# Six rows of the modulation leave the second half of the values and go to the output projection, whose last block gets a row beside each of six weight blocks

## The chip, the core and the metric

The kernel runs on one core of a Trainium2 chip. The metric is device time in microseconds (us) of one execution; lower is better. The engines are TensorE (PE; its weight loads are listed apart as PEld), VectorE (DVE), ScalarE (ACT), GpSimd (POOL) and SyncE (SP). Here SP issues nearly all loads, and POOL issues most stores. Every engine works through its own instructions in the order in which they were recorded, and waits on semaphores for the others; all DMAs of the core share 16 DMA engines.

## The reference

One layer of a diffusion backbone over 512 latent tokens with a prefix of 256 context tokens, width 2048. What matters here, cut down:

```python
mod_x = (silu(c) @ w_ada + b_ada)                       # 6 x 2048 numbers
sh1, s1, g1, sh2, s2, g2 = jnp.split(mod_x, 6, axis=-1)
h = rmsnorm(x, norm1_w) * (1 + s1) + sh1                # the same for the context
q, k, v (two kinds of heads) = projections of h         # v: "the values"
o = attention(q, k, v)                                  # 16 heads
x = x + g1 * (o @ w_o)                                  # "the output projection"
h2 = rmsnorm(x, norm2_w) * (1 + s2) + sh2
x = x + g2 * conv_ffn(h2)                               # w_up, convolution, SiLU, w_down
out = rmsnorm(x, final_w)
```

The modulation `mod_x` is a matrix times a vector: w_ada has 2048 x 12288 numbers, 100 MB, of which each is used once (a part also serves the context). All numbers are float32.

## The kernel before

**Matmuls.** Features lie on the 128 partitions, tokens along the free axis. A float32 product is made of three matmuls on rounded parts: ScalarE casts an operand to its high part (`wh`), VectorE subtracts that from the raw operand (`wr`) for the low part (`wl`), and TensorE adds high x high, high x low and low x high (lines 284 to 286, `mm3`). Weights come in blocks of 128 x 1024, 512 KB. Raw, high and low blocks have three buffers each, so that a load waits until the block three before it is cast and subtracted, and a cast until TensorE is done with the block three before.

**The modulation's rows.** The modulation isn't computed on TensorE but on VectorE, 128 features at a time. A "row" is one such piece: a load of 1024 KB of w_ada (128 x 2048, `ada`) and one instruction that multiplies it by silu(c), copied to all partitions (`cb`), and sums along it into one column of `modx`. There are 96 rows: 0 to 15 are sh1, 16 to 31 s1, 32 to 47 g1, 48 to 63 sh2, 64 to 79 s2, 80 to 95 g2. The rows of sh1 and s1 come first of all (those of s1 another way, through TensorE for both kinds of tokens). The rest is spread over later stages, always with two row buffers: a row's load waits until VectorE is done with the row two before it.

**Order of the stages, and where the rows are.**

1. Norms, first features, and the rows of sh1 and s1.
2. Features (keys, compressed queries): with each, 1 to 3 rows (`next_gemv`).
3. The values, in two halves of eight weight blocks (`values`). TensorE does 36 matmuls for a block; behind it come the cast and subtraction of a block for later, and then 0 to 2 rows on VectorE (`gate`), as a small table says. Each `gate` issues the load of one more row (`load_row`). The blocks that the second half loads last already belong to attention (`w_f`). At the end the results are split into two parts and written to DRAM, by POOL; the last four of these stores come out of the two row buffers, which are free by then.
4. Attention (`Flow`). A planner with a fixed table of due times orders the steps of all engines: loads of keys and values, projections of queries (`w_f` blocks, line 973 load, 985 cast, 986 subtraction), scores (line 1023), their maximum on VectorE (1026), the exponential on ScalarE (1028), the difference of the two maps (1177, 1178), rotary embedding (1124 to 1128), transposes and products with the values. At its end it also does the first quarter of the output projection.
5. The output projection `w_o`, in four groups of 512 features: group 0 within attention; groups 1 and 2 with one row for each of their 16 weight blocks (`next_gemv(wo, 1)`); and group 3, "the last block" of this document, eight weight blocks o0 to o7 written out by hand (`last_projection`) with no row before the change. For each of o0 to o5 TensorE does 24 matmuls, ScalarE casts the block after next (`cast(i + 2)`, line 1737), VectorE makes its low part (`low(i + 2)`, line 1745), which frees the raw buffer for another load (line 1558). o6 and o7 are done together, feature by feature, so that the next norm can begin.
6. The gated MLP: w_up, mostly by a recursion that saves multiplications, and w_down, to the end.

The stages 3, 4 and the last block onward are recorded by hand or by the planner: there the order on the engines is the order of the code. Groups 1 and 2 of the output projection stand outside, and the tile framework orders them.

**What reads the moved rows.** Rows 48 to 63 (sh2) are read in the second norm, after the last block; half of them also go into a small sum `db` (128 x 8), which was made on VectorE as soon as its inputs were there. g2 is read when w_down's first results come, g1 at the end of each group of the output projection.

Of the kernel before, what the change touches and what calls it, by code (L numbers as in the profile page):

```python
# [9 lines left out]
F32 = mybir.dt.float32  # L10
# [3 lines left out]
ALU = mybir.AluOpType  # L14
# [3 lines left out]
P = 128  # L18
D = 2048
# [201 lines left out]
def layer_kernel(ctx: ExitStack, tc: tile.TileContext, small, rope, c_row, cc_row, x_t, ctx_t, ada, ada_k,  # L221
                 w_g0, w_f, w_v, w_uqn, w_uqr, w_ukv, w_o, w_up0, w_up, w_dn, out_t):
    nc = tc.nc
    pe, ve, sc, gp = nc.tensor, nc.vector, nc.scalar, nc.gpsimd
# [8 lines left out]
    def nm(s):  # L233
        n[0] += 1
        return f"{s}{n[0]}"
# [64 lines left out]
    def col(name, j=0):  # L300
        o = OFF[name] + j
        return smt[:, o:o + 1]
# [8 lines left out]
    modx = cst.tile([P, 96], F32, name="modx")  # L311
# [52 lines left out]
    cb = st.tile([P, D], F32, name="cb")  # L364
# [6 lines left out]
    for j in (64, 96):  # L371
# [4 lines left out]
                            op1=ALU.mult)  # L376
# [3 lines left out]
    for i in range(2):  # L380
        o = OFF["lam"] + 128 * i
        ve.tensor_tensor_reduce(out=lt, in0=smt[:, o:o + 64], in1=smt[:, o + 64:o + 128], op0=ALU.mult,
                                op1=ALU.add, scale=1.0, scalar=0.0, accum_out=ls[:, i:i + 1])
# [64 lines left out]
    for p in range(8):  # L448
# [5 lines left out]
        def ctx_square(q=q, kts=kts, p=p):  # L454
            if p in ON_DVE:
                ve.tensor_tensor(hv(q(), kts, 1), cv(kts), cv(kts), op=ALU.mult)
            else:
# [3 lines left out]
             w=[q], hold=[cr[p // 2]])  # L461
# [34 lines left out]
    for k, (c0, c1) in enumerate(((0, T), (T, TT))):  # L496
# [13 lines left out]
            out=r, in0=nt[1]()[:, s], scalar=1.5, in1=r, op0=ALU.subtract, op1=ALU.mult), r=[nt[1]], w=[br])  # L510
# [222 lines left out]
    cb = kv.tile([P, D], F32, name="cb1")  # L733
# [2 lines left out]
    z = kv.tile([P, TT], F32, tag="lt", name=nm("z"), bufs=3)[:64]  # L736
    gp.memset(z, 0.0)
    gp.dma_start(zero_d, z)
    gv = iter([64 + i for i in range(16)] + [48 + i for i in range(16)] + [32 + i for i in range(16)])

    def next_gemv(pool, count):
        for _ in range(count):
# [159 lines left out]
    def values(half, vo):  # L902

        for kb in range(8):
            if half < 1 or kb < 7:
                raws.append(wload(next(wsrc)[0]))
            wh, wl = wready.pop(0)
            for j in range(2):
                kt = kb * 2 + j
                w = (wh[:, j * 512:(j + 1) * 512], wl[:, j * 512:(j + 1) * 512])  # L910
                order = (2, 3, 4, 5, 0, 1) if half and kt == KT - 1 else range(NKEY)
                for t in order:
                    src, o = (hx[kt], t * P) if t < 4 else (hc[kt], (t - 4) * P)
                    mm3(vo[t], (src[0][:, o:o + P], src[1][:, o:o + P]), w, kt == 0, kt == KT - 1)
            if not half and kb == 0:
                queries.pop(0)()
            wready.append(wsplit(raws.pop(0)))
            for _ in range(((2, 2, 2, 2, 2, 2, 2, 0), (2, 2, 2, 2, 2, 2, 1, 0))[half][kb]):
                gate()
            if queries and kb:  # L920
                queries.pop(0)()
        return order

    with tc.manual_schedule(engines={mybir.EngineType.PE, mybir.EngineType.Activation, mybir.EngineType.DVE,
# [4 lines left out]
        for half in range(2):  # L929
# [12 lines left out]
            for t in order:  # L942
                hl = []
                for _ in range(2):
                    if homes:
                        pool, g, bufs = homes.pop(0)
# [215 lines left out]
    for h in range(NH):  # L1162
        b, pace = BASE[h], SPANS[h] / 8
        ws = []
        for qt in range(NQT):
# [3 lines left out]
            for i in range(2):  # L1169
# [6 lines left out]
                out=second(), in0=rl()[:, 1:2], scalar1=neglam, scalar2=None, op0=ALU.mult), r=[rl], w=[second])  # L1176
            step("ACT", 0.85, t + 0.2, lambda p=ps[0], rl=rl: sc.mul(p(), p(), rl()[:, 0:1]), r=[rl], w=[ps[0]])
            step("DVE", 0.93, t + 1.2, lambda ps=ps, second=second: ve.scalar_tensor_tensor(
                out=ps[0](), in0=ps[1](), scalar=second(), in1=ps[0](), op0=ALU.mult, op1=ALU.add),
# [152 lines left out]
    for h in range(-1, NH):  # L1332
# [16 lines left out]
        p, i = h // 2, h % 2  # L1349
# [118 lines left out]
        ve.scalar_tensor_tensor(out=a2[:, dt:dt + 1], in0=modx[:, 64 + dt:65 + dt], scalar=1.0,  # L1468
                                in1=col("n2", dt), op0=ALU.add, op1=ALU.mult)
    db = sm.tile([P, 8], F32, name="db")  # L1470
    ve.tensor_tensor(db, modx[:, 56:64], modx[:, 48:56], op=ALU.add)

    HT = T // 2
    h0, h1 = slice(0, HT), slice(HT, T)
    halves = (h0, h1)
    x1, ss = [], wo.tile([P, T], F32, name="ss")
    gv = iter([80 + i for i in range(16)])

    def residual(dt):
        xr = wo.tile([P, T], F32, tag="xr", name=nm("xr"), bufs=4)  # L1480
        nc.sync.dma_start(xr, x_t[dt])
        x1.append(b2k())
        return xr
# [256 lines left out]
    def low(i):  # L1740
        if i < last and not kept_parts(i):
            hi, lo, raw, done = ready[i]
            n_ = 1024 // len(hi)
            for k, t in enumerate(lo):
                ve.tensor_tensor(t, raw[:, k * n_:k * n_ + n_], hi[k].bitcast(F32), op=ALU.subtract)  # L1745
            if done:
                done()
# [3 lines left out]
        return [tuple(h[j // k][:, j % k * P:j % k * P + P] for h in ready[i][:2]) for j in range(8)]  # L1751


    def last_projection(i):
        kb, w = jobs[i][1], [h[0] for h in ready[i][:2]]
        if kb < 6:
            for j in range(2):
                for d in range(4):
                    project(live["o"], d, kb * 2 + j, w, kb == 5 and j == 1 and d == 3)
            cast(i + 2)  # L1760
            low(i + 2)
            return
        outs, xr = live["o"], live["xr"]

# [341 lines left out]
    with tc.manual_schedule(engines={mybir.EngineType.PE, mybir.EngineType.Activation, mybir.EngineType.DVE,  # L2106
                                     mybir.EngineType.SP}):
        mem["ra"] = Ring(wp, "wr", 3, items_a)
        live["o"] = [b_tile() for _ in range(4)]
        live["xr"] = [residual(12 + d) for d in range(4)]  # L2110
        for i in range(2):
            cast(i)
            low(i)
        for i, job in enumerate(jobs):
            if job == ("n", 0):
                ps_b.release()
                ps_s.release()
                nb[0] = 3
                ps_b = tc.alloc_tile_pool(name="ps_m", bufs=3, space=PSUM, reuse_waits="tile")
                spare += [tp.tile([P, T], F32R, tag="tp", name=nm("tp")) for _ in range(8)]  # L2120
            {"o": last_projection, "n": first_tiles, "u": third_tile, "p": strassen, "d": strassen,
             "f": last_output}[job[0]](i)
# [86 lines left out]
```

## Time and profile before

| | |
|---|---|
| time, median of 3 runs | 2344.87 us (2342.84 to 2345.27) |
| the profiled execution's own time | 2342.02 us |
| its span (first to last instruction) | 2340.2 us |
| granted TensorE clock, mean | 0.993 of full |
| busy: PE, DVE, ACT, POOL | 2291.9, 1731.4, 1165.5, 268.0 us |
| DMA | 404.23 MB, mean 173 GB/s |
| values, second half | to about 423 us |
| output projection, last block | about 921 to 966 us |

How to read the rows that follow. The **page** lists each engine's busy time and share of the span. The list of **waits** has: who waited, for whom, us in total, times, the longest. A **timeline** row has: start, duration, engine, line, operation, tiles (written <- read), shape, count, and in brackets the engine's idle time before it and what ended that; SPq is SyncE issuing a DMA. A row of **windows** has: the stretch, its length, then for PE, PEld, DVE, ACT and POOL the busy time and (instructions), and at last the granted clock, the busy share of the DMA engines and GB/s. The **chain of waits** follows the work that ended last back from the end; its rows have start, duration and what the time went to, a DMA's from its issue to its landing. Rows of **groups** have a count, total busy time, mean ns of one, idle time before them. Rows of **DMA issues** end with KB of each and the median us from issue to landing.

### The profile page before, as it was taken

How to read it: one execution, taken by the hardware profiler on the slowest of the kernel's cores; microseconds unless marked ns; L12 is line 12 of the kernel's file. 1: busy time of each engine (PE TensorE's matmuls, PEld its weight loads, DVE VectorE, ACT ScalarE, POOL GpSimd, SP SyncE). 2: the span in 40 equal slices, each digit the busy share in tenths (PEclk: the TensorE clock that was granted, in tenths of full speed). 3: DMA queues.
4: the chain of work that ended last, by engine and by line, in shares of the span. 5: the costliest groups of instructions: out<-in, count | busy, mean ns of one | idle time of the engine just before them, and what ended most of it. 6: DMA issues, size and time to landing. Idle time of an engine off the chain costs nothing.

```text
span 2340.2 us, 32196 instructions
## 1 busy us (share of the span) xinstructions
PE 2291.9 (98%) x12378; PEld 1961.0 (84%) x12378; DVE 1731.4 (74%) x2206; ACT 1165.5 (50%) x1777; POOL 268.0 (11%) x308
## 2 busy tenths in 40 slices
PE   6999999899999999999999999999999999999998
PEld 4788888788888888898888888888888888888887
DVE  7988776698987776597685858585858585767667
ACT  6542211477767522455454545454545454545456
POOL 0000001100123222000101010101010101010110
PEclk8999999999999999999999999999999999999999
DMA  9978889745301197334647374646464555555573
GB/s 356 366 256 311 306 296 333 236 130 167 123 29 41 55 353 277 98 106 138 144 121 165 103 173 115 160 119 153 127 146 132 137 143 144 132 148 126 154 184 104
DMA packets 124731, 404.23 MB, mean 173 GB/s; under 512 B 14337, under 2 KB 18945, under 8 KB 114081
## 3 DMA queue, kind: packets, MB, share of 16 engines
q1 hardware_dynamic: 96658, 346.92, 44.4%
q0 software_dynamic: 26768, 54.21, 12.6%
q8 instruction: 97, 1.59, 0.3%
q10 hardware_dynamic: 1152, 1.05, 0.1%
q14 instruction: 56, 0.46, 0.1%
HBM read 332.45 MB, written 69.67 MB: 172 GB/s over the span
## 4 chain that ended last, share of the span: by engine, by line
PE 86%; DMA 5%; DVE 5%; issue 2%; ACT 1%; SPq 0%; POOL 0%; DVEq 0%; ACTq 0%; POOLq 0%
PE y L1921 13%; PE b L284 10%; PE b L285 10%; PE b L286 10%; PE y L1923 7%; PE z L1921 6%; PE s L1023 4%; PE z L1923 3%; PE x L1921 3%; DMA ada<-in_ada 2%; PE s L284 2%; PE s L286 2%; PE s L285 2%; PE x L1923 2%; PE f L284 2%
## 5 line engine op out<-in xcount | busy, mean ns | idle before, releaser
L1745 DVE TENSOR_TENSOR wl<-wr,wh 128x1024 fp32r<-128x1024 f32 x144 | 176.6, 1226 | 159.8 <-ACT wh L1737 159.1
L1942 POOL DMA_DIRECT2D x_d<-xs x160 | 139.8, 1001 | 1147.5 <-ACT xs L1941 1145.6
L1737 ACT CAST wh<-wr 128x1024 fp32r<-128x1024 f32 x144 | 150.9, 1048 | 217.0 <-PE b L285 117.9
L284 PE MATMUL b<-ah,wh 128*128 128x512 f32 (+1 forms) x664 | 256.8, 387 | 0.0
L285 PE MATMUL b<-al,wh 128*128 128x512 f32 (+1 forms) x664 | 256.7, 387 | 0.0
L286 PE MATMUL b<-ah,wl 128*128 128x512 f32 (+1 forms) x664 | 255.8, 385 | 0.0
L1745 DVE TENSOR_TENSOR wl<-rb,wh 128x1024 fp32r<-128x1024 f32 x123 | 150.1, 1220 | 121.0 <-ACT wh L1737 121.0
L1745 DVE TENSOR_TENSOR wl<-ws,wh 128x1024 fp32r<-128x1024 f32 x123 | 150.4, 1222 | 109.9 <-ACT wh L1737 109.9
L1737 ACT CAST wh<-rb 128x1024 fp32r<-128x1024 f32 x123 | 129.3, 1051 | 181.7 <-PE b L285 76.2
L1921 PE MATMUL y<-a2k,wh 128*128 128x512 f32 x656 | 164.0, 392 | 0.0
L1737 ACT CAST wh<-ws 128x1024 fp32r<-128x1024 f32 x123 | 128.5, 1044 | 68.5 <-PE b L285 48.5
L286 PEld LDWEIGHTS b<-ah,wl 128*128 128x128 f32 x664 | 124.8, 188 | 25.7
L284 PEld LDWEIGHTS b<-ah,wh 128*128 128x128 f32 x664 | 125.1, 188 | 22.9
L285 PEld LDWEIGHTS b<-al,wh 128*128 128x128 f32 x664 | 125.1, 188 | 21.9
L248 ACT CAST wh<-wr 128x1024 fp32r<-128x1024 f32 x51 | 53.5, 1052 | 169.4 <-DMA wr<-in_w_o 49.5
L1921 PEld LDWEIGHTS y<-a2k,wh 128*128 128x128 f32 x656 | 118.6, 189 | 21.6
L1026 DVE TENSOR_REDUCE m<-s 128x1 f32<-128x768 f32 x96 | 91.2, 952 | 25.5 <-PE s L1023 25.2
L1028 ACT ACTIVATE p<-s,m 128x768 f32<-128x768 f32 x96 | 86.8, 904 | 42.5 <-DVE m L1026 40.2
L352 DVE CUSTOM_DVE_ANT_0 ada<-ada,cb,smt 128x2048 f32<-128x2048 f32 x37 | 90.0, 2433 | 24.1 <-DMA ada<-in_ada 24.0
L1921 PE MATMUL y<-b2k,wh 128*128 128x512 f32 x410 | 106.8, 390 | 0.0
L1941 ACT ACTIVATE xs<-b,modx 128x512 f32<-128x512 f32 x160 | 101.2, 681 | 2.4 <-DMA x_d<-xs 2.1
L1923 PEld LDWEIGHTS y<-a2k,wl 128*128 128x128 f32 x656 | 89.5, 190 | 6.4
(528 smaller groups left out, 5943.8 us busy)
## 6 DMA issues: line engine op xcount, KB each, us to landing
ada<-in_ada SPq DMA_DIRECT2D x80, 1024.0 KB, 7.2
rb<-in_w_up SPq DMA_DIRECT2D x123, 512.0 KB, 4.4
wr<-in_w_dn SPq DMA_DIRECT2D x88, 512.0 KB, 3.8
x_d<-xs POOLq DMA_DIRECT2D x160, 256.0 KB, 6.0
wr<-in_w_up SPq DMA_DIRECT2D x53, 512.0 KB, 4.2
wr<-in_w_f SPq DMA_DIRECT2D x34, 512.0 KB, 6.8
adak<-in_ada_k SPq DMA_DIRECT2D x32, 512.0 KB, 7.7
wr<-in_w_o SPq DMA_DIRECT2D x32, 512.0 KB, 6.4
```

The source lines that it names most:

```text
L284: pe.matmul(out, st[0], mv[0], start=start, stop=False, **kw)
L285: pe.matmul(out, st[0], mv[1], start=False, stop=False, **kw)
L286: pe.matmul(out, st[1], mv[0], start=False, stop=stop, **kw)
L352: ve.tensor_tensor_reduce(out=junk, in0=w, in1=vec, op0=ALU.mult, op1=ALU.add, scale=1.0, scalar=col("b_ada", j), accum_out=dst[:, j:j + 1])
L1023: pe.matmul(s()[:, c0:c1], a, b[:, c0:c1], start=i == 0, stop=i == len(ms) - 1)
L1026: step("DVE", 0.87, t + cost + 0.2, lambda: ve.tensor_reduce(out=m(), in_=s()[:, :TT], axis=AX.X, op=ALU.max, negate=True), r=[s], w=[m])
L1737: sc.copy(t, raw[:, k * n_:k * n_ + n_])
L1745: ve.tensor_tensor(t, raw[:, k * n_:k * n_ + n_], hi[k].bitcast(F32), op=ALU.subtract)
L1921: pe.matmul(o, w[j][0], hs[j], start=start and j == 0, stop=False, skip_group_check=True)
L1923: pe.matmul(o[:, h0], w[j][1], hs[j][:, h0], start=False, stop=j == 7, skip_group_check=True)
L1941: sc.mul(x, po, modx[:, 80 + dt:81 + dt])
L1942: gp.dma_start(x1_d[dt], x, accum_op=ALU.add)
```

## The change

Three things move.

1. In the second half of the values the table of rows per block goes from 2, 2, 2, 2, 2, 2, 1, 0 to 2, 2, 2, 1, 0, 0, 0, 0. The list of rows for these stages loses rows 58 to 63.
2. The list for the output projection starts with these six rows, and then has g2's sixteen. The 16 blocks of groups 1 and 2 thus take rows 58 to 63 and 80 to 89, and six rows, 90 to 95, are left for the last block.
3. The last block gets two new helpers. `late_row` issues a load, `late_gate` does a row on VectorE and then issues another load. Two loads are issued ahead of o0, and one `late_gate` follows the subtraction in each of o0 to o5. The sum `db` is written down later, just ahead of the last block.

```diff
-    gv = iter([64 + i for i in range(16)] + [48 + i for i in range(16)] + [32 + i for i in range(16)])
+    gv = iter([64 + i for i in range(16)] + [48 + i for i in range(10)] + [32 + i for i in range(16)])
...
-            for _ in range(((2, 2, 2, 2, 2, 2, 2, 0), (2, 2, 2, 2, 2, 2, 1, 0))[half][kb]):
+            for _ in range(((2, 2, 2, 2, 2, 2, 2, 0), (2, 2, 2, 1, 0, 0, 0, 0))[half][kb]):
                 gate()
...
     db = sm.tile([P, 8], F32, name="db")
-    ve.tensor_tensor(db, modx[:, 56:64], modx[:, 48:56], op=ALU.add)
...
-    gv = iter([80 + i for i in range(16)])
+    gv = iter([58 + i for i in range(6)] + [80 + i for i in range(16)])
+    late_rows = []
...
+    def late_row():
+        j = next(gv, None)
+        if j is not None:
+            w = wo.tile([P, D], F32, tag="ada", name=nm("ada"), bufs=2)
+            nc.sync.dma_start(w, ada[j])
+            late_rows.append((j, w))
+
+    def late_gate():
+        j, w = late_rows.pop(0)
+        ve.tensor_tensor_reduce(out=w, in0=w, in1=cb, op0=ALU.mult, op1=ALU.add, scale=1.0,
+                                scalar=col("b_ada", j), accum_out=modx[:, j:j + 1])
+        late_row()
+
     def last_projection(i):
         kb, w = jobs[i][1], [h[0] for h in ready[i][:2]]
         if kb < 6:
...
             cast(i + 2)
             low(i + 2)
+            late_gate()
             return
...
         mem["ra"] = Ring(wp, "wr", 3, items_a)
         live["o"] = [b_tile() for _ in range(4)]
         live["xr"] = [residual(12 + d) for d in range(4)]
+        ve.tensor_tensor(db, modx[:, 56:64], modx[:, 48:56], op=ALU.add)
+        late_row()
+        late_row()
```

On TensorE, ScalarE and POOL the instructions stand in the same order as before. Three places differ.

SyncE at the end of the values, before: the last loads of rows (`ada`), of the values' and attention's first weight blocks, and then attention's first loads (`klz`, `qs`, `ks`).

```order
L893 DMA ada_3166<-in_ada 128x2048
L257 DMA wr_3168<-in_w_v 128x1024
L893 DMA ada_3211<-in_ada 128x2048
L893 DMA ada_3214<-in_ada 128x2048
L257 DMA wr_3216<-in_w_f 128x1024
L893 DMA ada_3259<-in_ada 128x2048
L257 DMA wr_3262<-in_w_f 128x1024
L1087 DMA klz_3394<-zero_d 64x768
L1097 DMA qs_3407<-q_d 128x512
```

The same place now:

```order
L257 DMA wr_3161<-in_w_v 128x1024
L257 DMA wr_3203<-in_w_f 128x1024
L257 DMA wr_3245<-in_w_f 128x1024
L1087 DMA klz_3376<-zero_d 64x768
L1097 DMA qs_3389<-q_d 128x512
```

The weight blocks follow each other directly, with no row's load, and so no wait for VectorE's rows, between them and ahead of attention's loads.

SyncE at the last block, before: the last of four loads of the residual (`xr`), then the weight blocks from o3 to the first of w_up.

```order
L1481 DMA xr_8441<-in_x_t 128x512
L1558 DMA wr_8448<-in_w_o 128x1024
L1558 DMA wr_8454<-in_w_o 128x1024
L1558 DMA wr_8484<-in_w_o 128x1024
L1558 DMA wr_8514<-in_w_o 128x1024
L1558 DMA wr_8544<-in_w_o 128x1024
L1558 DMA wr_8574<-in_w_up 128x1024
```

The same place now:

```order
L1481 DMA xr_8422<-in_x_t 128x512
L1758 DMA ada_8426<-in_ada 128x2048
L1758 DMA ada_8428<-in_ada 128x2048
L1558 DMA wr_8434<-in_w_o 128x1024
L1558 DMA wr_8440<-in_w_o 128x1024
L1558 DMA wr_8470<-in_w_o 128x1024
L1758 DMA ada_8473<-in_ada 128x2048
L1558 DMA wr_8503<-in_w_o 128x1024
L1758 DMA ada_8506<-in_ada 128x2048
L1558 DMA wr_8536<-in_w_o 128x1024
L1758 DMA ada_8539<-in_ada 128x2048
L1558 DMA wr_8569<-in_w_up 128x1024
```

Two rows stand ahead of o3, o4 and o5, and one each ahead of o6, o7 and the first two w_up blocks.

VectorE at the last block now, from the last eviction of group 2 (`b2k`) and the low parts of o2 to o5 (`wl`):

```order
L1487 SCALAR_TENSOR_TENSOR b2k_8395<-s_8104,modx,xr_8393 128x512
L1745 TENSOR_TENSOR wl_8467<-wr_8407,wh_8466 128x1024
L1763 ISA ada_8426,modx<-ada_8426,cb_7759,smt 128x2048
L1763 ISA modx 128x1
L1745 TENSOR_TENSOR wl_8500<-wr_8434,wh_8499 128x1024
L1763 ISA ada_8428,modx<-ada_8428,cb_7759,smt 128x2048
L1763 ISA modx 128x1
L1745 TENSOR_TENSOR wl_8533<-wr_8440,wh_8532 128x1024
```

Before, these subtractions followed each other with nothing between them; now a row (two instructions, the second stores the sum) stands behind each.

## The prediction

> **What bounds the kernel now.** The page first: TensorE is busy for 98% of the span, so only time in which TensorE waits, or runs at a lower clock, can be won. The list of TensorE's waits names one after the start-up phase that is longer than 2 us, and the table by windows puts it where the second half of the values hands over to attention:
>
> ```profile
> PE 2291.9 (98%) x12378; PEld 1961.0 (84%) x12378; DVE 1731.4 (74%) x2206; ACT 1165.5 (50%) x1777; POOL 268.0 (11%) x308
> PE s L1023 <- ACT p L1028: 6.0, 1, 6.0
> 400.00:410.00 10.00, 10.00 (x45) 8.27 (x45) 6.80 (x8) 1.06 (x1) 0.00 (x0) 1.00 0.90 325
> 430.00:440.00 10.00, 7.75 (x38) 6.34 (x36) 5.68 (x9) 3.61 (x7) 3.33 (x5) 1.00 1.03 397
> 443.00:444.00 1.00, 0.26 (x1) 0.26 (x2) 0.28 (x2) 0.69 (x2) 0.01 (x1) 0.50 1.01 399
> 448.00:449.00 1.00, 1.00 (x3) 0.74 (x3) 0.97 (x2) 1.00 (x3) 0.00 (x0) 0.50 0.07 16
> ```
>
> The last three columns are the granted clock, the DMA engines' share and GB/s. Up to 437 us TensorE is full while the DMA engines are full too; then it stands, and after the wait it runs at half clock. The timelines of TensorE and ScalarE and the chain of waits name the cause:
>
> ```profile
> 437.47 0.28 PE L1023 MATMUL s<-klz,qs 128*128 128x256 f32 x1
> 443.74 0.80 PE L1023 MATMUL s<-ks,qs 128*128 128x512 f32 x1 [6.00 <-ACT p L1028]
> 449.89 0.39 PE L1023 MATMUL s<-ks,qs 128*128 128x512 f32 x1
> 452.64 0.39 PE L1023 MATMUL s<-ks,qs 128*128 128x512 f32 x1
> ...
> 411.38 1.06 ACT L248 CAST wh<-wr 128x1024 fp32r<-128x1024 f32 x1 [8.21 <-DMA wr<-in_w_f]
> 435.52 0.93 ACT L1177 ACTIVATE p<-p,rl 128x768 f32<-128x768 f32 x1
> 441.75 1.04 ACT L985 CAST wh<-wr 128x1024 fp32r<-128x1024 f32 x1 [5.31 <-DMA wr<-in_w_f]
> 442.70 0.90 ACT L1028 ACTIVATE p<-s,m 128x768 f32<-128x768 f32 x1
> 444.59 0.90 ACT L1028 ACTIVATE p<-s,m 128x768 f32<-128x768 f32 x1 [0.90 <-DVE rt L1128]
> 447.60 0.90 ACT L1028 ACTIVATE p<-s,m 128x768 f32<-128x768 f32 x1
> ...
> 426.34 15.39 DMA wr<-in_w_f
> ```
>
> The exponential p (L1028) frees the scores' bank, but stands on ScalarE behind the cast of a w_f block, and that block takes 15.39 us to land. It is issued late and lands late because the queue was behind. SyncE's timeline:
>
> ```profile
> 400.89 2.75 SPq L893 DMA_DIRECT2D ada<-in_ada  x2
> 408.48 0.33 SPq L893 DMA_DIRECT2D ada<-in_ada  x1
> 409.40 0.52 SPq L1087 DMA_DIRECT2D klz<-zero_d  x1
> 426.34 2.76 SPq L973 DMA_DIRECT2D wr<-in_w_f  x2
> ```
>
> Attention's first load (409.40) stands behind the last gate row (408.48), which waits until VectorE has emptied a row buffer.
>
> **The change in the second half of the values: the wait.** It takes away six gate rows, 1024 KB and one VectorE instruction each:
>
> ```profile
> L898 DVE CUSTOM_DVE_ANT_0 ada<-ada,cb,smt 128x2048 f32<-128x2048 f32 x27 | 63.3, 2350 | 16.6 <-DMA ada<-in_ada 16.4
> ```
>
> VectorE's 6 x 2.35 = 14.1 us are worth nothing as such, since TensorE has 10.00 of 10 us in that stage. What counts is the queue: 6 x 1.049 = 6.3 MB, at the 325 GB/s of 400 to 410 us 19 us of transfers. With nothing waiting for rows, the two w_f blocks and attention's loads leave as soon as casts free their buffers, which TensorE paces; I estimate 10 to 15 us sooner. The block of 426.34 takes the buffer of the first w_f block, so its load can leave once that one is cast; that cast (411.38) waited 8.21 us for DMA, and when TensorE alone paces it, is due by 407 (the values end at 423; 36 matmuls to a block at 45 per 10 us are 8 us, and the cast may start two blocks before the end). The block is then there well before 436.45, when ScalarE (435.52 + 0.93) is free for its cast.
>
> Sum for this place. (a) From the cast's start to TensorE's restart it was 443.74 - 441.75 = 1.99 us; from 436.45 that gives 438.44, so 5.30 us are saved and 0.7 us of waiting stays. (b) Half clock: from 443.74 to 449.89 TensorE did one set of scores and 12 projection matmuls; one set and 9 matmuls at full clock are 452.64 - 449.89 = 2.75 us, with three more of 0.23 us 3.45. It took 6.15: 2.70 saved. (c) Given back: the neighbours rested during the wait and now are tight. VectorE:
>
> ```profile
> 439.27 0.69 DVE L1124 TENSOR_TENSOR rt<-f,ropet 128x512 f32<-128x512 f32 x1 [1.00 <-DMA v_d<-v]
> 441.25 0.95 DVE L1026 TENSOR_REDUCE m<-s 128x1 f32<-128x768 f32 x1
> ```
>
> L1124 writes where the values lay and waits for their store; without that 1.00 us the maximum (L1026) ends at 441.2, its exponential starts at 441.25 and TensorE's next scores at 442.3 (1.04 us from exponential to scores, 442.70 to 443.74). TensorE would be there at 438.44 + 3.45 = 441.9: 0.4 us of waiting. The next exponential follows 3.01 us later (444.59 to 447.60), scores 2.75 us later: 0.25 more; VectorE's chain to the one after, with a subtraction and three products ahead of its maximum, adds about 0.3 (an estimate). Together 0.95. Net 5.30 + 2.70 - 0.95 = 7.05 us. Bounds: 8.7 if nothing is left (6.00 + 2.70); 2.6 if only the last row's 1.05 MB at 397 GB/s comes off the block's landing and the half clock stays.
>
> **The clock.** A wait of 1.02 us elsewhere left the clock alone, 6.00 us did not:
>
> ```profile
> 967.85 0.70 PE L1809 MATMUL s<-sq,ones 128*128 128x256 f32 x2 [1.02 <-ACT sq L1773]
> 966.00:968.00 2.00, 0.98 (x8) 0.77 (x8) 1.89 (x5) 0.77 (x2) 0.36 (x1) 1.00 0.00 0
> ```
>
> The remaining 0.7 us is nearest the first, so (b) counts in full. [...]
>
> **The change in the output projection: the cover.** Rows 58 to 63 take the places of six gate-2 rows in the two middle blocks one for one (nothing there changes), so six rows come new into the last block, o0 to o7, one behind each of o0 to o5. Two are issued ahead of the loop, in front of o3's weights. What stands there now:
>
> ```profile
> 930.17 1.05 ACT L1737 CAST wh<-wr 128x1024 fp32r<-128x1024 f32 x1 [6.42 <-DMA wr<-in_w_o]
> 931.90 1.05 ACT L1737 CAST wh<-wr 128x1024 fp32r<-128x1024 f32 x1 [0.67 <-PE b L286]
> 937.14 1.05 ACT L1737 CAST wh<-wr 128x1024 fp32r<-128x1024 f32 x1 [4.20 <-PE b L285]
> 942.59 1.05 ACT L1737 CAST wh<-wr 128x1024 fp32r<-128x1024 f32 x1 [4.38 <-PE b L285]
> ...
> 931.25 1.23 DVE L1745 TENSOR_TENSOR wl<-wr,wh 128x1024 fp32r<-128x1024 f32 x1 [7.08 <-ACT wh L1737]
> ...
> 860.00:870.00 10.00, 10.00 (x46) 8.29 (x45) 6.18 (x6) 2.11 (x2) 0.00 (x0) 1.00 0.98 375
> 905.00:910.00 5.00, 5.00 (x24) 4.14 (x23) 4.36 (x4) 1.06 (x1) 0.00 (x0) 1.00 1.02 403
> 920.00:925.00 5.00, 5.00 (x24) 4.14 (x23) 3.12 (x3) 2.77 (x4) 4.97 (x5) 1.00 0.93 299
> ...
> ada<-in_ada SPq DMA_DIRECT2D x80, 1024.0 KB, 7.2
> ```
>
> A block is 5.45 us (937.14 to 942.59). o3's weights arrive at 930.17, their low part is ready at 932.48 and first read in o3's third matmul, about 937.8: 5.3 us of slack. Two rows are 2.1 MB, 5.2 us at 403 GB/s, and some of it fits into 920 to 925, where only 299 were moved. So o3 just arrives: 0 us, 1.2 us if the rows run at 325 GB/s. Behind it each block adds 2.35 us to VectorE's 1.23, 3.6 of 5.45 us. On VectorE the next block's subtraction stands behind each row, and two blocks later TensorE needs it; on SyncE o6, o7 and the first w_up blocks stand behind the loads of rows 3 to 6, needed at 942.59 and then 5.45 us apart. Two buffers bring two rows per 7.2 + 2.35 = 9.55 us, 4.8 per row, under 5.45. The row of 860 to 870 is this same load (one row, one block) with TensorE at 10.00. I take 0, nearest that row; bounds 0 and 13.8 (D).
>
> From 919 to 954 us the stage now moves 6.3 MB (four 256 KB loads and stores each, eight weight blocks); with the rows 12.6 MB in 35 us, 360 GB/s. [...] The sum db moves on VectorE and costs 0.17 us in cover of either stage.
>
> **Sum.** The profiled execution took 2342.02 us, 1.8 around its span; 2342.0 - 7.0 = 2335.0. It lies 2.85 under the median of the runs, so that the median becomes 2344.87 - 7.0 = 2337.9.
>
> **The rivals.**
> B, the backlog goes only in part: 2.6 us, 2342.3. For it: attention's own loads and the values' stores fill the engines too (397 GB/s from 430 to 440, when no row is left). Against: two of the six rows' loads were issued at 400.89 and one at 408.48, right ahead of them.
> C, a new wait takes the old one's place. The second exponential (444.59) writes into the freed row buffers, which still hold values on their way out; POOL stores them last:
>
> ```profile
> 430.77 0.75 POOL L955 DMA_DIRECT2D v_d<-ada  x1 [3.29 <-DMA v_d<-nr]
> 434.23 0.75 POOL L955 DMA_DIRECT2D v_d<-ada  x1 [0.33 <-issue]
> v_d<-ada POOLq DMA_DIRECT2D x4, 256.0 KB, 10.1
> ```
>
> 434.23 + 10.1 = 444.3, so this store, not L1128, ends that wait. Unchanged it would hold the scores to 445.6, 4.3 us before the old 449.89; 1.6 with half clock. Say 3: 2341.9. Against: the stores queue behind the same backlog, and are needed only by 441.2.
> D, slower: in the last block the two row buffers fall into step, so that rows 3 to 6 come one per 9.55 us and each holds VectorE's subtraction: 4 x (9.55 - 5.45) = 16.4, less the 5.3 of slack, plus 2.7 at half clock: 13.8 - 7.05 = 6.7 slower, 2351.6. It decides once a row takes over 2 x 5.45 - 2.35 = 8.55 us to land. Against: 7.2 is the median, and from 860 to 870 this load cost TensorE nothing.
> E, nothing: SyncE's order, and casts that TensorE paces, hold the w_f block, and it lands no sooner: 2344.9. Against: the cast that frees its buffer waited 8.21 us for DMA itself.
>
> **How the numbers follow.** Forecast 0.74, B 0.08, C 0.08, D 0.05, E 0.05. The forecast's own range is 5.5 to 8.7 us, 2336.2 to 2339.4, and with the runs' spread (2342.84 to 2345.27) 2335.0 to 2340.6. Stretched over B's and C's centres: 2335.0 to 2342.6. What can be told from no change is 0.2%, 4.7 us: faster 0.74 (the forecast, whose own range begins above it), same 0.21 (B, C, E), slower 0.05 (D).
>
> **What would show it.** Right: no L1023 wait over 1 us between 430 and 460, granted clock 1.00 there, DMA share well under 1 before 420, the second L985 cast waiting on no DMA; and TensorE at 10.00 per 10 us through the last block, with o3's cast some 4 us later. Wrong: a wait on v_d stores at the second exponential (C), a w_f cast still idle on DMA (B, E), or TensorE waiting for L1737 or L1745 (D).

## The result, and the profile after

| | before | after |
|---|---|---|
| median | 2342.84 us (7 runs, 2339.07 to 2348.64, measured beside the change) | 2333.48 us (7 runs, 2332.54 to 2337.57) |
| profiled execution | 2342.02 us, span 2340.2 | 2333.48 us, span 2331.6 |
| granted clock, mean | 0.993 | 0.995 |

The ratio is 0.996, with a 95% interval of 0.9948 to 0.9972: faster by 7 to 12 us. The prediction had 2337.9 (2335.0 to 2342.6): the direction is right, the size is not. One run of before, among those measured beside the experiments, took 4242.98 us at a granted clock of 0.807 and is left out everywhere.

The page of the profile after, a row of its list of TensorE's waits and its table by windows:

```profile
PE 2289.3 (98%) x12378; PEld 1958.4 (84%) x12378; DVE 1729.4 (74%) x2206; ACT 1164.8 (50%) x1777; POOL 267.4 (11%) x308
PE s L1023 <- ACT p L1028: 0.7, 1, 0.7
400.00:410.00 10.00, 10.00 (x46) 8.29 (x45) 1.22 (x1) 1.05 (x1) 0.00 (x0) 1.00 1.04 226
430.00:440.00 10.00, 9.13 (x44) 7.31 (x43) 7.29 (x13) 6.13 (x11) 0.94 (x2) 1.00 0.00 1
440.00:460.00 20.00, 19.81 (x99) 16.22 (x98) 18.97 (x28) 16.45 (x30) 1.13 (x4) 1.00 0.41 112
```

The wait of 6.0 us at the scores is 0.7 us, the clock stays at full, and from 430 to 440 us, where 397 GB/s were moved before, the DMA engines have nothing left to do. A new wait of 0.5 us stands in the last block (L1745, shown further below). From 400 to 410 us the DMA engines are as full as ever (1.04): what changed is what they carry. Timelines of after, SyncE, POOL, ScalarE and TensorE, and a row of its DMA issues:

```profile
392.27 0.52 SPq L1087 DMA_DIRECT2D klz<-zero_d  x1
408.62 6.57 SPq L973 DMA_DIRECT2D wr<-in_w_f  x2
424.77 2.98 POOL L955 DMA_DIRECT2D v_d<-ada  x4
433.67 1.04 ACT L985 CAST wh<-wr 128x1024 fp32r<-128x1024 f32 x1
434.70 0.90 ACT L1028 ACTIVATE p<-s,m 128x768 f32<-128x768 f32 x1
435.74 0.50 PE L1023 MATMUL s<-ks,qs 128*128 128x512 f32 x1 [0.68 <-ACT p L1028]
439.75 0.39 PE L1023 MATMUL s<-ks,qs 128*128 128x512 f32 x1
...
v_d<-ada POOLq DMA_DIRECT2D x4, 256.0 KB, 4.0
```

Attention's first load leaves at 392.27 (before: 409.40), the w_f block at 408.62 (426.34). Its cast at 433.67 waits for nothing. The values' last stores, which POOL had to issue from 430.77 to 434.23, leave together from 424.77 on and take 4.0 us instead of 10.1.

Where the 8.6 us between the spans are: I compare the start of the same matmul in both profiles. Late in the start-up, in code that the change doesn't touch, in before and in after; then, in after, the last matmul ahead of the scores that waited (437.47 in before):

```profile
155.43 2.08 PE L839 MATMUL s<-c4k,wl 128*128 128x256 f32 x16
...
152.75 2.08 PE L839 MATMUL s<-c4k,wl 128*128 128x256 f32 x16
434.78 0.28 PE L1023 MATMUL s<-klz,qs 128*128 128x256 f32 x1
```

At 155 us after leads by 2.68 us already (437.47 - 434.78 = 2.69 just ahead of the hand-over). At the scores that waited, its lead is 443.74 - 435.74 = 8.00; at the next it is 449.89 - 439.75 = 10.14, and 9.87 is left at 446 us of after. So the hand-over brought 7.18 us, and 2.69 came from the start-up. The rest of attention and the two middle groups take 0.20 us of it in small pieces: at 927 us of after the lead is 9.67. Then the last block takes some back. The matmul that read o3's low part, before, and the rows around it after (SyncE, the first row on VectorE, o3's cast and low part, TensorE, a window, and the row of the chain of waits):

```profile
937.63 0.39 PE L286 MATMUL b<-a2k,wl 128*128 128x512 f32 x1
...
913.20 1.01 SPq L1758 DMA_DIRECT2D ada<-in_ada  x2
914.32 1.68 SPq L1558 DMA_DIRECT2D wr<-in_w_o  x3
922.28 2.35 DVE L1763 CUSTOM_DVE_ANT_0 ada<-ada,cb,smt 128x2048 f32<-128x2048 f32 x1 [7.79 <-DMA ada<-in_ada]
926.32 1.05 ACT L1737 CAST wh<-wr 128x1024 fp32r<-128x1024 f32 x1 [12.25 <-DMA wr<-in_w_o]
927.41 1.23 DVE L1745 TENSOR_TENSOR wl<-wr,wh 128x1024 fp32r<-128x1024 f32 x1 [2.76 <-ACT wh L1737]
928.69 0.50 PE L286 MATMUL b<-a2k,wl 128*128 128x512 f32 x1 [0.53 <-DVE wl L1745]
915.00:920.00 5.00, 5.00 (x23) 4.14 (x23) 0.00 (x0) 0.00 (x0) 2.46 (x3) 1.00 0.87 285
914.32 11.93 DMA wr<-in_w_o
```

The two rows issued at 913.20 take until 922 and beyond, at 285 GB/s, and o3's weights behind them 11.93 us. The low part comes 0.53 us late by the row, and the lead falls to 937.63 - 928.69 = 8.94 at once and to 8.81 with the next matmuls: 0.86 less. Another 0.25 us goes in the MLP, nearly all of it at about 1900 us, where nothing was changed. 2.69 + 7.18 - 0.20 - 0.86 - 0.25 = 8.6.

### The profile page after: what moved, and what is told of

It reads as the page before. It is cut to its first block, busy times and chain, and to the rows that moved or that the text cites. A ratio compares the mean times of both kernels' runs of the same rounds, so it can differ in the third digit from the quotient of the medians.

```text
span 2331.6 us, 32185 instructions
## 1 busy us (share of the span) xinstructions
PE 2289.3 (98%) x12378; PEld 1958.4 (84%) x12378; DVE 1729.4 (74%) x2206; ACT 1164.8 (50%) x1777; POOL 267.4 (11%) x308
## 4 chain that ended last, share of the span: by engine, by line
PE 92%; DVE 5%; DMA 1%; ACT 1%; issue 1%; SPq 0%; DVEq 0%; ACTq 0%
PE y L1935 13%; PE b L284 11%; PE b L285 10%; PE b L286 10%; PE y L1937 7%; PE z L1935 6%; PE s L1023 4%; PE z L1937 3%; PE s L284 3%; PE s L285 3%; PE s L286 3%; PE x L1935 3%; PE x L1937 2%; PE f L284 2%; PE f L285 1%; PE f L286 1%
## 5 line engine op out<-in xcount | busy, mean ns | idle before, releaser
L1745 DVE TENSOR_TENSOR wl<-wr,wh 128x1024 fp32r<-128x1024 f32 x144 | 176.5, 1226 | 139.8 <-ACT wh L1737 139.0
L1745 DVE TENSOR_TENSOR wl<-rb,wh 128x1024 fp32r<-128x1024 f32 x123 | 150.1, 1220 | 121.0 <-ACT wh L1737 121.0
L1745 DVE TENSOR_TENSOR wl<-ws,wh 128x1024 fp32r<-128x1024 f32 x123 | 150.3, 1222 | 109.5 <-ACT wh L1737 109.5
L1028 ACT ACTIVATE p<-s,m 128x768 f32<-128x768 f32 x96 | 86.8, 904 | 44.8 <-DVE m L1026 43.5
```

## The experiments

Two things were to be told first: whether the start-up's 2.69 us are chance, and whether the hand-over's gain comes from the values' part alone while the late rows cost about 1 us. The other runs ask how much has to be moved for the gain, and which waiting instruction sets it. The column "hand-over" is how many microseconds TensorE loses there against the profile of after, from the start of the same matmul (at 424 and at 460 us of after); "last block" is the same from 927 to 957 us, given as the loss against the kernels without any late row there.

| kernel | median us (runs) | ratio to before, 95% | hand-over | last block |
|---|---|---|---|---|
| before once more | 2344.08 (11) | 0.9998 to 1.0015 | 11.1 | 0 |
| values part alone | 2333.20 (5) | 0.9945 to 0.9971 | 0 | 0 |
| late part alone | 2343.53 (12) | 0.9997 to 1.0016 | 7.3 | 1.6 |
| rows behind o3, o4 | 2334.19 (7) | 0.9955 to 0.9979 | 0 | 0 |
| the same again | 2333.50 (6) | 0.9941 to 0.9965 | 0 | 0 |
| after once more | 2334.66 (5) | 0.9942 to 0.9966 | 0 | 2.4 |
| one row moved | 2343.91 (11) | 0.9987 to 1.0004 | 9.8 | 0 |
| three rows moved | 2342.07 (11) | 0.9979 to 0.9996 | 8.4 | 0.7 |
| one row, buffers turned | 2340.11 (11) | 0.9980 to 0.9999 | 4.3 | 0 |
| two rows | 2336.78 (7) | 0.9960 to 0.9982 | 1.7 | 1.0 |
| four rows | 2333.84 (5) | 0.9949 to 0.9974 | 0 | 0.2 |
| before, buffers turned | 2344.12 (11) | 0.9996 to 1.0014 | 10.1 | 0 |

In the profile of before the hand-over cost 7.1 against after by this measure, and after lost 0.9 in the last block. The medians of before beside these runs are 2343.2 (24 runs), 2344.05 (22) and 2343.2 (23).

**Before once more.** No edit.

> The kernel before, once more, as a measure of chance. In the two profiles TensorE reached the first features 2.6 us apart (the first group of L839 matmuls at 155.60 us before, at 152.91 us after the change), although the code up to there is the same. Theory 1: that is chance between executions. Then this kernel's mark may lie anywhere from 152 to 157 us, the ratio to before is 1.000 within its interval, and the wait of 6.0 us with the half clock is at its old place. Theory 2: the 2.6 us belong to the change (another program, another start). Then the mark here is 155.6 within 0.5 us, and every changed kernel below has 152.9.

The start-up was 2.3 us quicker than in the first profile of before, with the same code. The hand-over was worse. TensorE's timeline:

```profile
428.81 0.47 PE L1023 MATMUL s<-ks,qs 128*128 128x512 f32 x1 [2.99 <-DMA klz<-k_d]
445.71 0.79 PE L1023 MATMUL s<-ks,qs 128*128 128x512 f32 x1 [5.36 <-ACT p L1028]
```

Besides the wait for the exponential there is one for a load of keys, and 11.1 us are lost against after where the first profile lost 7.1. The start-up's lead of after is chance, by this and the other runs: the matmul at 155.43 in before starts between 152.06 and 154.36 in the thirteen other profiles, whatever the kernel. The first profile of before had the slowest start of all fourteen, and a mild hand-over.

**The values part alone.** The table of rows as changed, and no late rows: rows 58 to 63 are computed nowhere.

```diff
-    gv = iter([58 + i for i in range(6)] + [80 + i for i in range(16)])
+    gv = iter([80 + i for i in range(16)])
+    ve.memset(modx[:, 58:64], 0.0)
...
-            late_gate()
...
-        late_row()
-        late_row()
```

> The first part alone: rows 58 to 63 are left out altogether (their six columns are zeroed at the start), the output projection has its old sixteen rows and its last block none. Theory 1: the gain at the hand-over to attention is here in full, 7.2 us from TensorE's L1023 at 443.74 to the same one after 449.89, and the 0.9 us that TensorE lost at o3's low part is saved: 7.2 us less than before in the trace after allowance for the start, 1.0 to 1.2 us less than the changed kernel. Rival: the late rows cost nothing, and this kernel has the changed kernel's time within 0.3 us. Theory 2 would add 2.6 us in the start-up.

```profile
440.00:460.00 20.00, 19.80 (x99) 16.23 (x98) 18.97 (x28) 16.57 (x31) 1.51 (x5) 1.00 0.40 112
```

The window reads as in after (19.81), there is no wait at L1745, and the median is after's within 0.3 us: the gain is the values' part. Of the 1.0 to 1.2 us that this kernel was to be faster than after, the median doesn't show more than that 0.3.

**The late part alone.** The values as before; six rows that the two middle blocks have already done are done a second time in the last block.

```diff
-            for _ in range(((2, 2, 2, 2, 2, 2, 2, 0), (2, 2, 2, 1, 0, 0, 0, 0))[half][kb]):
+            for _ in range(((2, 2, 2, 2, 2, 2, 2, 0), (2, 2, 2, 2, 2, 2, 1, 0))[half][kb]):
...
-    gv = iter([58 + i for i in range(6)] + [80 + i for i in range(16)])
+    gv = iter([80 + i for i in range(16)] + [80 + i for i in range(6)])
```

> The second part alone: the values keep their 27 rows, and the last block of the output projection does rows 80 to 85 a second time as its six late rows (db stands where the change has it). Theory 1: the wait of 6.0 us and the half clock stay; TensorE waits about 0.5 us for o3's low part and loses 0.9 us there in all: 0.9 us slower than before, 0 to 2. Rival (the price forecast): 0, no wait for L1745. Rival D of the prediction: 6 us or more slower than before.

```profile
443.98 0.80 PE L1023 MATMUL s<-ks,qs 128*128 128x512 f32 x1 [7.36 <-ACT p L1028]
937.60 0.50 PE L286 MATMUL b<-a2k,wl 128*128 128x512 f32 x1 [0.53 <-DVE wl L1745]
```

The wait at the hand-over is back, at 7.36 us, and o3's low part is late by the same 0.53 us as in after. By the median it is before.

**Rows behind o3 and o4.** The first two late rows are issued after the loads of o3 and o4.

```diff
-        late_row()
-        late_row()
         for i in range(2):
             cast(i)
             low(i)
+        late_row()
+        late_row()
```

> The change, with the first two late rows issued behind the weights of o3 and o4 instead of ahead of them (after the casts of o0 and o1). Theory 1: the two rows in the queue ahead of o3 are what TensorE waits for; o3's cast goes from 926.3 back to about 921, no wait for L1745, and the kernel is 0.9 us faster than the changed one, 7.2 us under before after allowance for the start. Rival: the rows only push the lateness on to o5, which now stands behind them, and the time is the changed kernel's within 0.3 us.

```profile
917.88 1.05 ACT L1737 CAST wh<-wr 128x1024 fp32r<-128x1024 f32 x1 [4.60 <-DMA wr<-in_w_o]
```

o3's cast comes 8.4 us earlier than in after (7.7 when both are set against the same matmul of TensorE), and TensorE doesn't wait at L1745. The median isn't lower than after's, though, so the comparison was made once more, beside after.

> The changed kernel once more, unchanged. Theory 1 (the long wait at the hand-over is gone for good, and what is left varies with the start-up alone): profile with at most two waits of TensorE at L1023 of 0.5 to 1.1 us and full clock from 440 to 460 us, the short wait of about 0.5 us for o3's low part (L1745) again, median 2333.5 +- 1. Theory 2 (after's profile was a lucky execution, as the profile of before was a mild one): a wait over 3 us at L1023, median 2335 to 2338.

> The kernel whose late rows are loaded behind the weights of o3 and o4, once more, beside the changed kernel on the same chip. If the two rows ahead of o3's weights cost the 0.9 to 1.2 us that the traces show, its median is lower than the changed kernel's by about 1 us and its trace has no wait at L1745 in the last block; if that wait is made up for later (the next stages have slack for it), the two are within 0.5 us.

Both hand-overs were those of after. In the last block of after once more, o3 was nearly in time, and then the later rows held up the subtractions; timelines of VectorE and TensorE there:

```profile
943.40 2.35 DVE L1763 CUSTOM_DVE_ANT_0 ada<-ada,cb,smt 128x2048 f32<-128x2048 f32 x1 [1.29 <-DMA ada<-in_ada]
945.68 1.22 DVE L1745 TENSOR_TENSOR wl<-wr,wh 128x1024 fp32r<-128x1024 f32 x1
946.96 0.50 PE L286 MATMUL b<-a2k,wl 128*128 128x512 f32 x1 [0.55 <-DVE wl L1745]
955.89 1.13 PE L1820 MATMUL s<-ss,ones 128*128 128x512 f32 x2 [0.87 <-POOL ss L1807]
```

A row waits for its load, the subtraction behind it starts late, and TensorE waits for that. With the wait at the next norm, whose inputs VectorE makes behind the last of these rows, 2.4 us are lost. The two kernels' medians together are 2333.8 (12 runs of the change) and 2334.0 (13 with the rows behind): the loss is in the traces, but a difference of 1 us isn't to be seen in runs that spread from 2331.6 to 2337.7.

**One row and three rows moved.** The table of the second half is 2, 2, 2, 2, 2, 2, 0, 0 with one late row, or 2, 2, 2, 2, 2, 0, 0, 0 with three; the edit for one row is shown. In both the late rows are loaded ahead of o3's weights, as in the change: in the run with three rows nothing puts them behind o3 and o4, as its expectation has it.

```diff
-            for _ in range(((2, 2, 2, 2, 2, 2, 2, 0), (2, 2, 2, 1, 0, 0, 0, 0))[half][kb]):
+            for _ in range(((2, 2, 2, 2, 2, 2, 2, 0), (2, 2, 2, 2, 2, 2, 0, 0))[half][kb]):
...
-    gv = iter([58 + i for i in range(6)] + [80 + i for i in range(16)])
+    gv = iter([63 + i for i in range(1)] + [80 + i for i in range(16)])
...
+        if not late_rows:
+            return
```

> Only the last of the six rows is moved (the one whose load was issued at 408.48, right ahead of attention's first load at 409.40); the other five stay in the second half of the values, and the output projection's last block has one late row, ahead of o3's weights. Order theory (what cost was the place of one row load, which holds the queue until VectorE frees a buffer): attention's first load is issued some 4 us sooner, the w_f block lands in time for its cast at 436.4, and nearly the whole gain is there: wait at L1023 under 1.5 us, full clock, no wait at L1745 in the last block, median about 2334 to 2335. Volume theory (what cost was the bytes in front of the w_f block): one row's 1.05 MB is a sixth of the volume, so 1.2 us of the 7 if the gain is proportional, 2.6 us if the block lands earlier by this row's transfer and the half clock stays: median 2340.5 to 2342, a wait of 3 to 5 us at L1023 and half clock behind it.

> The last three of the six rows are moved, three stay; in the last block the three late rows are loaded behind the weights of o3 and o4. Order theory: the full gain at the hand-over, as with one row (wait under 1.5 us, full clock), and nothing lost in the last block: median 2333 to 2334. Volume theory, proportional: half of the gain, wait of about 3 us with half clock behind it, median about 2338 to 2340; with 2.6 us per row: the full gain, and then one row (the run beside it) must show about a third of it.

Both missed: with three rows moved nearly the whole gain is absent. The timelines of ScalarE and TensorE, one row first:

```profile
442.26 0.90 ACT L1028 ACTIVATE p<-s,m 128x768 f32<-128x768 f32 x1 [10.46 <-DMA v_d<-ada]
443.31 0.80 PE L1023 MATMUL s<-ks,qs 128*128 128x512 f32 x1 [8.01 <-ACT p L1028]
...
439.41 0.90 ACT L1028 ACTIVATE p<-s,m 128x768 f32<-128x768 f32 x1 [7.62 <-DMA v_d<-ada]
441.13 1.03 ACT L985 CAST wh<-wr 128x1024 fp32r<-128x1024 f32 x1
440.45 0.80 PE L1023 MATMUL s<-ks,qs 128*128 128x512 f32 x1 [5.17 <-ACT p L1028]
```

The cast waits for nothing any more; an exponential waits instead, for the values' last stores, the mechanism of the prediction's rival C. But it is the third exponential of attention, where rival C had the fifth (444.59 in before). The cause is the number itself. The two row buffers take turns; the last values get the one that is next; and the exponentials' outputs lie over both. (The four last stores all come out of that one buffer, not out of both as said ahead of the prediction.) An odd number of rows gives the values the buffer that the third exponential needs. The two runs had changed two things at once, so the next ones keep the number even, or turn the buffers back.

**One row, two rows, four rows.** The first turns the buffers by a one-column write; the others have the tables 2, 2, 2, 2, 2, 1, 0, 0 and 2, 2, 2, 2, 1, 0, 0, 0. Here too the late rows stand ahead of o3's weights, though the expectations for two and four rows say behind.

```diff
+                        ve.memset(kv.tile([P, D], F32, tag="ada", name=nm("ada"), bufs=2)[:, :1], 0.0)
                         row_home = kv.tile([P, 4, 4, P], F32R, tag="ada", name=nm("ada"), bufs=2)
```

> One row moved, as in the run with one row, but the two row buffers are turned by one place (a one-column memset on VectorE takes the next buffer just before the last values get theirs), so that the values' last stores leave the buffer that the fifth exponential of attention needs, as in before, and not the third. Theory 1 (each waiting instruction has its own slack; the run with one row lost its gain to the third exponential, which waited for these stores): the w_f block of the run with one row landed at 437.8 and the stores at 442.2, so about 4.5 us of waiting at L1023 behind the block and 1 to 2 us more at the fifth exponential: median about 2341. Order theory: the full gain, 2334 to 2335. Proportional theory (a sixth of the gain per row): 2342.5.

> The last two of the six rows moved, loaded behind the weights of o3 and o4. An even number, so that the fifth exponential, not the third, stands behind the values' last stores. Theory 1 (slack): by the landings with one and with three rows (w_f block 437.8 and 430.2, stores 442.2 and 439.3) the block lands by about 434, in time, and the stores by about 440.7, some 2 us late for the fifth exponential: no long wait behind the cast, a wait of about 2 us, full clock, median 2336 to 2337.5. Proportional theory: a third of the gain, 2341.

> The last four rows moved, loaded behind the weights of o3 and o4. Theory 1 (slack): the block has long landed and the stores are there for the fifth exponential: waits at L1023 of at most 1 us, full clock, median 2333.5 to 2334.5, the gain of all six. Proportional theory: two thirds of the gain, 2337.6.

ScalarE and TensorE with one row (the added line makes L1028 there L1029, L1023 L1024 and so on); with two, VectorE's L1124, two waits of TensorE's with the exponential between them, and SyncE at the last block; and the fifth exponential with four:

```profile
439.03 1.04 ACT L986 CAST wh<-wr 128x1024 fp32r<-128x1024 f32 x1 [3.77 <-DMA wr<-in_w_f]
441.02 0.79 PE L1024 MATMUL s<-ks,qs 128*128 128x512 f32 x1 [4.46 <-ACT p L1029]
...
435.23 1.04 ACT L985 CAST wh<-wr 128x1024 fp32r<-128x1024 f32 x1
437.83 0.69 DVE L1124 TENSOR_TENSOR rt<-f,ropet 128x512 f32<-128x512 f32 x1 [0.68 <-DMA v_d<-v]
439.22 0.50 PE L284 MATMUL f<-a4k,wh 128*128 128x512 f32 x1 [0.94 <-DVE rt L1125]
441.97 0.90 ACT L1028 ACTIVATE p<-s,m 128x768 f32<-128x768 f32 x1 [4.72 <-DMA v_d<-ada]
443.02 0.50 PE L1023 MATMUL s<-ks,qs 128*128 128x512 f32 x1 [0.78 <-ACT p L1028]
916.39 0.98 SPq L1758 DMA_DIRECT2D ada<-in_ada  x2
917.47 18.27 SPq L1558 DMA_DIRECT2D wr<-in_w_o  x5
...
439.26 0.91 ACT L1028 ACTIVATE p<-s,m 128x768 f32<-128x768 f32 x1 [2.78 <-DVE m L1026]
```

With one row moved the w_f block is still late, with a wait of 4.46 us behind it. With two the cast is free, and what is late waits for the values' stores: first L1124, for a store out of another buffer (TensorE's lag behind after grows by 0.76 us there), then the fifth exponential, as in rival C (0.94 us more, 1.7 in all). With four, it waits for VectorE like after's, and nothing is lost. The medians 2340.1, 2336.8 and 2333.8 are those that the slack of each waiting instruction gave (2341, 2336 to 2337.5, 2333.5 to 2334.5), within 1 us. In proportion to the rows they would have been 2342.5, 2341 and 2337.6. The runs with one row spread from 2334.2 to 2345.4, so that there the 95% interval (2338.5 to 2343.0) holds both; with two and with four rows it leaves the proportion out. That the place of the last row in the queue is what counts, as the prediction argued against rival B, falls: with that one row gone, most of the gain is missing. In the last block the order of loads now decides, over all the runs together. In all six executions with two rows ahead of o3's weights (after, after once more, late part alone, two, three and four rows) TensorE loses time there, 0.2 to 2.4 us; with one row ahead of them (two executions) or two behind o3 and o4 (two) it loses none. Set against the same matmul in the values part alone, o3's cast comes 5.4 to 6.3 us later with two rows ahead, 3.2 to 3.3 with one, and 0.7 to 1.6 earlier with the rows behind. In the executions whose only loss is at o3, the loss follows this delay: 0.2 us with 5.4, 0.7 with 5.9, 0.9 with 6.1, 1.0 with 6.2.

**Before with its buffers turned.** Only the write of the last diff, put into before.

> The kernel before with all its rows; only the two row buffers are turned by one place by the one-column memset, so that the third exponential of attention, not the fifth, stands behind the values' last stores. This is the third way of the prediction (rival C) by itself. Theory 1: the third exponential, at 434.6 in before, waits for the stores, which land between 442 and 444.5; the cast that was late is then hidden behind it; TensorE waits 8 to 10 us at L1023, and the median is 1 to 3 us over before: 2345 to 2347. If the stores did not matter: no change, 2344.

```profile
441.68 0.90 ACT L1029 ACTIVATE p<-s,m 128x768 f32<-128x768 f32 x1 [6.35 <-DMA v_d<-ada]
443.40 1.03 ACT L986 CAST wh<-wr 128x1024 fp32r<-128x1024 f32 x1
442.72 0.80 PE L1024 MATMUL s<-ks,qs 128*128 128x512 f32 x1 [5.18 <-ACT p L1029]
```

The third exponential waits for the stores, as expected, but the time is before's (0.9996 to 1.0014), not 1 to 3 us more. The w_f block would have come about then anyway: its cast behind this exponential has no wait of its own at 443.40, and in before it started at 441.75, in before once more at 443.7. The two late things, both behind the same DMA backlog, cost here no more than one (2344.12 us against 2343.2). By this, making only one of them early in this kernel would win little; that was not run, but the kernel with three rows moved is close to it: the block is there at 430.2, the stores land at 439.3, and 8.4 us are lost.

## Why the prediction was right or wrong

**The cause, right.** The backlog of transfers at the hand-over (397 GB/s from 430 to 440 us) held attention, and with six rows out of it the cast (433.67 for 441.75) and the stores (issued from 424.77 for 430.77 on) are early. Each sign named for it came: the wait under 1 us, the clock at 1.00, the second cast without a DMA ahead of it. "DMA share well under 1 before 420" didn't come (1.04 from 400 to 410): attention's loads themselves moved there.

**The sum at this place, right against the execution it was made from.** Less the 2.69 us of the start, TensorE restarts 8.00 - 2.69 = 5.31 us sooner (a: 5.30). From there to the lead of 9.87 it gains 1.87 more (b and c: 2.70 - 0.95 = 1.75); it gives back 0.56 by the next scores and then 0.27, where (c) had 0.4 and 0.55. Together 7.18 against 7.05.

**The last block, mis-sized.** The step "so o3 just arrives: 0 us" failed: after lost 0.9, after once more 2.4, the late part alone 1.6. Of the signs named for the last block neither came as forecast: TensorE waited for L1745, and o3's cast was 6 us late, not 4. The two rows were to cost o3's weights 5.2 us against 5.3 of slack; they cost 5.4 to 6.3. The 403 GB/s was taken from a stage of loads alone, and the 299 of 920 to 925 us was counted as room, but with the rows there no more was moved in that stretch (282 and 285 GB/s from 910 to 920 us of after). That the block's stores are the reason was not tested. Rival D's mechanism (a row that is late holds the subtraction behind it) is real, in the row of 943.40 with 1.29 us of waiting; its size of 13.8 us is not: in that execution three rows waited for their loads, 3.42, 1.29 and 0.81 us, where D had four, each 4.1 us late.

**The time, wrong.** The profiled execution after lies 1.5 us under its forecast of 2335.0: the start's 2.69 and the hand-over's 0.13 on one side; attention's 0.20, the last block's 0.86 and the MLP's 0.25 on the other. That it comes so near is in part luck, since the start-up's share is chance. The step that failed for the median (2337.9 forecast, 2333.5 measured) is "so that the median becomes 2344.87 - 7.0". Of the 4.4 us, 2.0 lie in the base, a median of only three runs (2344.87; the seven runs beside the change gave 2342.84, and all 76 give 2343.5), and 2.4 in the gain (9.4 for 7.0). The step took the wait of one execution for the usual one. The same hand-over lost 7.1, 11.1 and 7.3 us in three executions, and the runs of before spread from 2338 to 2349 us, while 27 of the 35 runs of the kernels without the backlog lie between 2332 and 2335.2. Over all runs the medians differ by 9.7 us (2343.5 and the 2333.8 of the change's 12 runs); the executions looked at explain 7 to 11 of hand-over, less 0.9 to 2.4 in the last block. Where the rest lies, and why the backlog is worse in one execution than in the next, isn't settled.

**The rivals.** B and E are out: the cast is not idle for DMA after. But B's price of one row alone, 2.6 us, is close to what that row brought (2343.2 - 2340.1 = 3.1, with the buffers turned back, though the interval reaches from 0.2 to 4.7). C did not come, since with all six rows gone the stores land by 431, for an exponential that runs at 438.47; with two rows gone it came, at 0.9 us for the 3 that I had.

## What to carry to other kernels

Here a stage that ended with full DMA engines (a share of 1.03 from 430 to 440 us of before) handed its delay to several instructions of the next, each with a slack of its own: list all of them with their slack, because the gain came as they came free one after another (3.1 us with one row and the buffers turned, 6.4 with two, 9.4 with four and 9.4 with six), not in proportion to the bytes, and making only one of two late ones early won little (2.0 us with three rows, whose cast was early and whose stores were not). The wait for the backlog varied from run to run (by 4.0 us in three executions of the same code, as the start-up did by 3.4 in fourteen), so one profile gave its mechanism but not its usual size; a second profile of the unchanged kernel told the two apart. Where buffers took turns, a change of their count moved who waited for whom (the third exponential, by 10.46 us, with one row; the fifth, by 4.72, with two): keep the parity, or test for it.

## What was not expected of the hardware

The half clock came in steps. Windows of one microsecond, for one row with buffers turned, for three rows and for before once more; the third column from the right is the granted clock:

```profile
440.00:441.00 1.00, 0.00 (x0) 0.00 (x0) 0.85 (x1) 0.97 (x3) 0.00 (x0) 0.77 1.01 390
443.00:444.00 1.00, 1.00 (x4) 0.81 (x3) 1.00 (x2) 1.00 (x3) 0.00 (x0) 0.52 0.02 6
...
438.00:439.00 1.00, 0.00 (x0) 0.00 (x0) 0.00 (x0) 0.00 (x0) 0.00 (x0) 0.96 0.11 41
449.00:450.00 1.00, 1.00 (x6) 0.81 (x5) 0.97 (x2) 1.00 (x3) 0.00 (x0) 0.92 0.00 0
...
430.00:431.00 1.00, 1.00 (x4) 0.76 (x4) 0.74 (x1) 0.00 (x0) 0.61 (x2) 0.61 1.01 393
433.00:434.00 1.00, 1.00 (x6) 0.85 (x5) 0.71 (x1) 1.00 (x3) 0.77 (x2) 0.69 1.02 394
```

With 1 at full and 0.5 at half, the first falls at 440.54 and rises at 443.96, 3.42 us; the second falls at 438.92 and rises at 449.16, 10.24 us, three times as long. In before it is two steps (442.56 to 449.38, 6.82). The fall came 2.9 to 4.8 us into the long wait in the seven executions that had one. A step followed a shorter wait too: in before once more TensorE stood only from 425.82 to 428.81 (2.99 us), and the clock was at half from 430.22 to 433.62, while TensorE was busy again. Counted in stretches of 3.41 us (half of before's 6.82) back and forth from each fall, the clock fell after stretches in which TensorE, by the profile, was busy for 0 to 41%, and stayed at full after 59% or more; it rose after 86% or more, and stayed at half after 77% or less. How long the clock stayed at half after TensorE's restart did not follow the length of the wait: 5.64 us behind the 6.00 of before, 3.06 us behind the 7.36 of the late part alone, where the clock rose at 447.04. A second short wait went with one more step: behind first waits of 5.17 and 5.18 us (three rows; before, buffers turned) a wait of 1.00 us left the second stretch at half clock 77 and 71% busy, and the clock came back after three steps, where single waits of 5.36 to 7.36 us took two.
